# Where the sample stage's queries, constants, first keys and cache copies are issued, in a hybrid RG-LRU and windowed-attention step

## The chip, the core and the metric

The kernel runs on one core of a Trainium2 chip. The metric is the device time of one execution in microseconds (us), as the median of repeated runs. One execution was recorded by the hardware profiler; all rows below are from it. Engines are called PE (matrix products), DVE (vector), ACT (scalar functions), POOL (general) and SP, which in this kernel only issues transfers (DMAs). POOL and ACT issue DMAs too.

## The reference

One mixer layer is computed for a prompt of 2048 tokens and for 8 sequences with 8 new tokens each, which have caches. Cut to what matters:

```python
def dilated_group_sample(q, k, v, kv_buf, bias, dil):
    L = kv_buf.shape[1]                       # 128, 512, 2048 for the groups 0, 1, 2
    kc = jnp.concatenate([kv_buf[:, :, 0], k], axis=1)
    vc = jnp.concatenate([kv_buf[:, :, 1], v], axis=1)
    idx = L + jnp.arange(T)[:, None] - dil * jnp.arange(129)[None, :]   # dil 1, 4, 16
    s = jnp.einsum('bthe,btjhe->bthj', q, kc[:, idx]) * ATTN_SCALE + bias.T
    p, lse = softmax_stats(s, valid)
    o = jnp.einsum('bthj,btjhe->bthe', p, vc[:, idx])
    new_buf = jnp.stack([kc, vc], axis=2)[:, T:]      # the cache, shifted by 8 tokens
    return o, lse, new_buf

def mixer_layer(...):
    z = rms_norm(x, g_norm) @ w_in            # split in xa, ga, q, k, v, gb, gm
    hs, h_last = rg_lru(causal_conv(xa), h0, ...)
    ya = (hs * silu(ga)) @ w_lru_proj
    # three groups of 4 heads: banded attention for the prompt, the above for the samples
    yb = (merge of the groups * silu(gb)) @ w_attn_proj
    gates = sigmoid(gm + b_merge)
    y = x + (gates[:1024] * ya + gates[1024:] * yb) @ w_out
```

The caches of the samples are inputs, and the caches shifted by the 8 new tokens are outputs.

## The kernel before

The kernel is one hand-ordered program: each engine takes its instructions in the order of the code, and semaphores order the engines among each other. Its stages follow one another in time:

- The attention stage, 0 to about 1130 us: 12 heads of 17 units each (the loop variable is `i`). PE projects and computes the banded attention of the prompt.
- The gate of the attention output, then eight RG-LRU blocks, to about 1652 us.
- `gm_block(f)` for f = 0 to 15, to about 2061 us. Each f computes 128 of the merge gates' columns in five column tiles: 24 matmuls (`zT`, L763) into a PSUM tile, a sigmoid by ACT (L992), which empties the tile into gt, and a store to DRAM (Gsc, issued by ACT). Four PSUM tiles take turns. The weights of each f are loaded on SP (`wzr`, L683), cast by ACT and split by a subtraction on DVE (`wz`, L94 and L95). Between the tiles stands the attention of the samples: for f of 1 and more, one entry of the list `plan` is taken after each tile and its functions are called. The stretch f = 1 to 15 (1675 to 2061) is called the sample stage here.
- The output projections (L1424, L1480, L1512), to the end.

The attention of the samples has these pieces. `kmake` makes the key products of a group: `init` loads the first keys (kt, L156), `queries` loads the queries (qs, L146), and `go` does two products on DVE (kjk, L179), and loads the next keys. In the sample stage the group is 0, with four query tiles at first and four more in `go`, which go into the same buffers. `sload` and `sload_k` load scores of the new tokens and of the cached keys that other stages computed (SA, L1057, L1058; SCt, L1040, L1047). `scores` and `news` (L1066, L1072, L1075) put them together on DVE, with the constants MK, NI and relb, which `prep` loads. `v2_p` copies the normalised P for the values of group 2 (L1126). `v2_load(n)` loads cached values into one of six buffers (v, L1145), `v2_mul(n)` multiplies them by P on ACT (L1149), and `v2_acc(n)` adds them on DVE (L1155). `v1_p` sends P of group 1 through DRAM (PSC, L1134, on POOL). `v_conv` casts and splits values that `v_mm` multiplies on PE (vt, then OT at L1214).

`copy()` issues one of 184 transfers from a cache to its output (L110, on SP; 176 of them have 480 KB). It is called at fixed places of the attention stage, of the RG-LRU blocks and of `gm_block`, and does nothing when none is left. Before the change 94 are issued in the attention stage, 80 in the RG-LRU blocks, five in `gm_block(0)` and five in `gm_block(1)`.

The lines that issue the transfers at the beginning of the sample stage are these:

```python
    sload(2)
    sload_k(2)
    prep()
    for i in range(6):
        v2_load(i)
    G.kq = kmake(mp, 0, 2)
    plan += [[] for _ in range(70)]
    ...
    at_(1, G.kq.init, G.kq.queries)
```

Of the kernel before, what the change touches and what calls it, by code (L numbers as in the profile page):

```python
# [21 lines left out]
NS = 64  # L22
# [12 lines left out]
def raw(ap, off, dims):  # L35
    return bass.AP(ap.tensor, ap.offset + off, dims)
# [6 lines left out]
def program(tc, I, O, C, upto=99, debug=False):  # L43
    nc = tc.nc
    es = ExitStack()
    G = K()
# [4 lines left out]
    PE, ACT, DVE, POOL = nc.tensor, nc.scalar, nc.vector, nc.gpsimd  # L51
    dma = nc.sync.dma_start
# [9 lines left out]
    QS = sd("QS", [3, NS, 512])  # L62
# [16 lines left out]
    def pool(stack, name, **kw):  # L79
        return stack.enter_context(tc.tile_pool(name=name, bufs=1, reuse_waits="tile", **kw))  # L80
# [26 lines left out]
    def copy(n=1):  # L107
        for _ in range(n):
            if copies:
                i = dma(*copies.pop())  # L110
                if not G.manual:
                    tc.keep_in_program_order(i)
# [4 lines left out]
    def kmake(p, g, ntile):  # L117


        q = K()  # L120
        q.g = g
        q.SC = p.tile([128, 256], F32, name="SCk", tag="SCk", bufs=1)
        jk = p.tile([128, 128], mybir.dt.bfloat16, name="kjk", tag="kjk", bufs=1)
        kts, qts = {}, {}
        if g == 2:
            seq = [(n, 0) for n in range(64)]
            out = lambda n, t, h: h * 64 + n
        elif g == 1:
            seq = [(n, t) for n in range(32) for t in range(2)]
            out = lambda n, t, h: t * 128 + h * 32 + n  # L130
        else:
            seq = [(n, t) for half in range(2) for n in range(8) for t in range(half * 4, half * 4 + 4)]
            out = lambda n, t, h: t * 32 + h * 8 + n
        tiles = [seq[i][0] for i in range(len(seq)) if i == 0 or seq[i][0] != seq[i - 1][0]]

        def q_load(t):
            tag, bufs = ("qb", "q4")[t % 2] if g == 0 else "qs", (2, 2, 1)[g]
            qts[t] = p.tile([128, 512], F32, name="qs", tag=tag, bufs=bufs)
            if g == 2:
                for a in range(2):  # L140
                    dma(qts[t][a * NS:(a + 1) * NS], QS[2])
            elif g == 1:
                for b in range(8):
                    dma(qts[t][b * 16:(b + 1) * 16], raw(QS, (NS + b * 8 + 4 * t) * 512, [[0, 4], [512, 4], [1, 512]]))
            else:
                dma(qts[t], raw(QS, t * 512, [[8 * 512, 8], [0, 16], [1, 512]]))  # L146

        def k_load(i):
            if i < len(tiles):
                n = tiles[i]  # L150
                kts[i] = p.tile([128, 512], F32, name="kt", tag="kv", bufs=ntile)
                if g == 2:
                    for a in range(2):
                        dma(kts[i][a * NS:(a + 1) * NS], G.cache[2][:, (n * 2 + a) * 16:(n * 2 + a) * 16 + 8, 0].rearrange("b t h e -> b t (h e)"))
                else:
                    dma(kts[i], G.cache[g][:, n * 16:(n + 1) * 16, 0].rearrange("b t h e -> b t (h e)"))  # L156

        q.n, q.tile, q.half, q.left = 0, 0, 0, 2 * len(seq)

        def init():  # L160
            for i in range(ntile):
                k_load(i)

        def queries():
            for t in range((4, 2, 1)[g]):
                q_load(t)

        def go():
            q.left -= 1
            n, t = seq[q.n]  # L170
            if q.half == 0 and q.n and seq[q.n - 1][0] != n:
                q.tile += 1
                kts.pop(q.tile - 1)
            if q.half and q.tile and seq[q.n - 1][0] != n:
                k_load(q.tile + ntile - 1)
            for h in ((0, 1), (2, 3))[q.half]:
                c = slice(h * 128, (h + 1) * 128)
                o = out(n, t, h)
                DVE.tensor_tensor_reduce(jk, kts[q.tile][:, c], qts[t][:, c], 1.0, 0.0, ALU.mult, ALU.add, q.SC[:, o:o + 1])  # L179
            if g == 0 and q.half and 28 <= q.n < 32:  # L180
                q_load(t + 4)
            q.half ^= 1
            if q.half == 0:
                q.n += 1
            if q.left == 0:
                dma(SCs[g], q.SC)
        q.init, q.queries, q.go = init, queries, go
        return q
# [113 lines left out]
    def w_load(hd_, k):  # L302
        g, h = hd_
        hd = g * 4 + h
        wr = ap_.tile([128, 384], F32, name="wr", tag="wraw", bufs=4)
        src = win[k * 128:(k + 1) * 128, C_Q:C_GB].rearrange("p (s c) -> p s c", s=3)[:, :, hd * HD:(hd + 1) * HD]
        dma(wr.rearrange("p (s c) -> p s c", s=3), src)
        Wr[hd_, k] = wr
# [227 lines left out]
    for i in range(N + 3):  # L536
# [91 lines left out]
        if nh:  # L628
# [11 lines left out]
            if ph == 13:  # L640
# [1 line left out]
                w_conv(nh, 1, DVE)  # L642
                w_load(nh, 4)
                w_load(nh, 5)
        if i > 17 and i % 2:
            copy()
        if i == 115:
            k_flush()
# [368 lines left out]
    mp = pool(sms, "mp")  # L1017
    BF16 = mybir.dt.bfloat16
    relb = mp.tile([NS, 96], F32, name="relb")
    NI = mp.tile([NS, 11, NS], BF16, name="NI")  # L1020
    MK = mp.tile([NS, 3, NS], BF16, name="MK")
# [4 lines left out]
    Zc = [None]  # L1026

    def prep():
        dma(relb, I["rel_bias"][0:8].rearrange("b h -> (b h)").unsqueeze(0).to_broadcast([NS, 96]))
        dma(NI, C["ni"])  # L1030
        dma(MK, C["mk"])
        dma(SEL, C["sel"])
        for z in Zs:
            POOL.memset(z.bitcast(F32), 0.0)

    def sload_k(g):
        S = SCg[g] = mp.tile([NS, 512], F32, name="SCt", tag="PT")
        if g == 2:
            for a in range(2):
                dma(S[:, a * 256:(a + 1) * 256], SCs[2, a * NS:(a + 1) * NS])  # L1040
            return
        for t in range(8):
            if g == 1:
                src = SCs[1].rearrange("(b m r) (u c) -> u r b m c", b=8, r=4, u=2)[t // 4, t % 4]
            else:
                src = SCs[0].rearrange("(b s) (t c) -> t b s c", b=8, t=8)[t]
            dma(S[t:NS:8].rearrange("b (m c) -> b m c", c=(32, 128)[g]), src)  # L1047

    def sload(g):
        SA = SAs[g] = mp.tile([NS, 4, 192], F32, name="SA", tag="SA", bufs=2)  # L1050
        br = SA[:, :, 0:128]
        o = g * 4 * 128 * NBX + 127
        if g == 0:
            for h in range(4):
                dma(br[:, h], raw(Dsc, o + h * 128 * NBX, [[0, 8], [NBX - 1, 8], [1, 128]]))
        else:
            dma(br, raw(Dsc, o, [[0, NS], [128 * NBX, 4], [1, 128]]))  # L1057
        dma(SA[:, :, 128:192], SN[g * 4:g * 4 + 4].rearrange("h p k -> p h k"))  # L1058
# [63 lines left out]
    SEL = mp.tile([128, 2, NS], F32, name="SEL")  # L1122
# [14 lines left out]
    def v2_load(n):  # L1137
        if n < 96:
            v2s[n] = mp.tile([128, 4, 128], F32, name="v2", tag="v2", bufs=6)
        if 64 <= n < 96:  # L1140
            dma(v2s[n].rearrange("p h e -> p (h e)"), G.cache[1][:, (n - 64) * 16:(n - 63) * 16, 1].rearrange("b t h e -> b t (h e)"))
        if n < 64:
            for a in range(2):
                src = G.cache[2][:, (n * 2 + a) * 16:(n * 2 + a) * 16 + 8, 1].rearrange("b t h e -> b t (h e)")
                dma(v2s[n][a * NS:(a + 1) * NS].rearrange("p h e -> p (h e)"), src)  # L1145
# [119 lines left out]

    sload(2)
    sload_k(2)
    prep()
    for i in range(6):
        v2_load(i)  # L1270
    G.kq = kmake(mp, 0, 2)
    plan += [[] for _ in range(70)]

    def at_(n, *fs):
        plan[n].extend(fs)
# [3 lines left out]
    while len(kts) < G.kq.left:  # L1279
        t = kts[-1] if kts else 3  # L1280
# [11 lines left out]
        at_(mmt[i] - 1, P(v_conv, i))  # L1292
    T = mmt[-1]
    assert T + 1 < 68
    at_(1, G.kq.init, G.kq.queries)
    for i in range(2):
        at_(1 + i, P(states, i))
    at_(2, P(scores, 2), P(news, 2, range(4)), P(sload, 1), P(sload_k, 1))
# [5 lines left out]
    for i in range(98):  # L1304
        t = 6 + i * 60 // 98
# [296 lines left out]
```

## Time and profile before

| what | before |
|---|---|
| median of 3 runs | 2537.51 us (2537.02 to 2538.25) |
| the profiled execution, its own time | 2537.17 us |
| its span, first to last instruction | 2535.4 us |
| mean granted clock of PE | 0.995 |
| PE, DVE, ACT, POOL busy | 2482.5, 1543.3, 1081.6, 557.1 us |
| PE idle in the sample stage (1675 to 2061) | 386.00 - 363.45 = 22.55 us |

The span is the time between the first and the last recorded instruction; the execution's own time is 1.8 us longer. Busy times are sums over the span, and an engine that is busy part of the time can still be the one that another waits for at one place. The granted clock is a share of PE's full clock: 1.00 is 2.4 GHz, 0.50 is 1.2 GHz.

### The profile page before, as it was taken

The numbers are of one execution on the slowest core, as the hardware profiler recorded it, in microseconds if no ns is written. First come the engines' busy times: TensorE is split into PE (matmuls) and PEld (weight loads), VectorE is DVE, ScalarE is ACT, GpSimd is POOL, SyncE is SP. The second block draws the span as 40 slices with busy tenths as digits, with TensorE's granted clock in tenths as the row PEclk, the third lists the DMA queues.
The fourth block names the chain that finished last, engine by engine and source line by source line (L and its number), as shares of the span: only waits on it lengthen the run. The fifth ranks groups of instructions, "written<-read, shape, count | busy, mean of one in ns | idle before, by whom it ended". The sixth has DMA issues, their size and how long they took to land. (4 is left out here: it accounts for less than half of the span.)

```text
span 2535.4 us, 44585 instructions
## 1 busy us (share of the span) xinstructions
PE 2482.5 (98%) x15178; PEld 2337.5 (92%) x15178; DVE 1543.3 (61%) x4805; ACT 1081.6 (43%) x3318; POOL 557.1 (22%) x889
## 2 busy tenths in 40 slices
PE   7999999999999999999999999998998999999999
PEld 7999999999999999999999898997898899989988
DVE  6744686777786777646676677735776623433322
ACT  5633454443554443444465655544566511211110
POOL 3423322222212221213233343320000112200000
PEclk9999999999999999999999999999999999999999
DMA  5453564554553443327734333445664589533332
GB/s 145 118 123 99 140 187 136 163 167 143 160 162 106 123 118 96 111 73 227 216 131 156 130 116 124 141 136 192 193 206 153 160 234 333 188 107 127 109 123 67
DMA packets 311000, 376.30 MB, mean 148 GB/s; under 512 B 54912, under 2 KB 254639, under 8 KB 307932
## 3 DMA queue, kind: packets, MB, share of 16 engines
q1 hardware_dynamic: 285076, 338.42, 44.3%
q0 software_dynamic: 14176, 17.71, 2.6%
q10 hardware_dynamic: 11520, 17.31, 1.9%
q8 instruction: 120, 1.97, 0.3%
q14 instruction: 108, 0.88, 0.1%
HBM read 295.45 MB, written 168.33 MB: 183 GB/s over the span
## 5 line engine op out<-in xcount | busy, mean ns | idle before, releaser
L336 PE MATMUL z<-w,RH 128*128 128x384 f32 (+1 forms) x3088 | 888.7, 349 | 4.9 <-POOL w L317 1.7
L763 PE MATMUL zt<-RH,wz 128*128 128x384 f32 (+2 forms) x2560 | 700.6, 357 | 14.2 <-ACT gt L992 8.6
L336 PEld LDWEIGHTS z<-w,RH 128*128 128x128 f32 (+1 forms) x3088 | 553.2, 188 | 14.0 <-POOL w L317 5.9
L763 PEld LDWEIGHTS zt<-RH,wz 128*128 128x128 f32 x2560 | 466.3, 190 | 59.7 <-ACT gt L992 10.3
L336 PE MATMUL z<-w,RL 128*128 128x384 f32 x1544 | 520.8, 337 | 0.1
L763 PE MATMUL zt<-RL,wz 128*128 128x384 f32 (+2 forms) x1280 | 455.0, 355 | 0.0
L336 PEld LDWEIGHTS z<-w,RL 128*128 128x128 f32 x1544 | 291.7, 189 | 0.8 <-DVE RL L95 0.5
L763 PEld LDWEIGHTS zt<-RL,wz 128*128 128x128 f32 x1280 | 243.1, 190 | 22.3
L179 DVE CUSTOM_DVE_ANT_0 kjk<-kt,qs 128x128 bf16<-128x128 f32 x768 | 226.7, 295 | 60.3 <-DMA kt<-in_cache_kv_w 19.4
L408 ACT ACTIVATE P<-P,o 128x128 f32<-128x128 f32 (+1 forms) x192 | 88.9, 463 | 312.7 <-DVE o L407 312.7
L345 ACT ACTIVATE jk<-z 128x128 bf16<-128x128 f32 (+1 forms) x408 | 112.8, 277 | 249.4 <-PE trc L376 185.4
L95 DVE TENSOR_TENSOR KQ<-trc,KQ 128x256 fp32r<-128x256 f32 x192 | 81.4, 424 | 199.0 <-ACT KQ L94 198.8
L347 POOL TENSOR_SCALAR ss<-ss 128x2 f32<-128x2 f32 (+1 forms) x204 | 44.6, 219 | 706.0 <-ACT jk L345 663.2
L1480 PEld LDWEIGHTS zt<-y1t,w_wlo 128*128 128x128 f32 x1536 | 190.3, 192 | 0.6
L1480 PE MATMUL zt<-y1t,w_wlo 128*128 128x256 f32 (+1 forms) x1536 | 190.6, 287 | 0.0
L1512 PE MATMUL zt<-w_wo,mt 128*128 128x512 f32 x672 | 162.0, 395 | 0.0
L1512 PEld LDWEIGHTS zt<-w_wo,mt 128*128 128x128 f32 x672 | 126.2, 188 | 30.4
L348 POOL TENSOR_TENSOR rs<-ss,neghalf 128x2 f32<-128x2 f32 (+1 forms) x204 | 142.3, 697 | 17.0
L1149 ACT ACTIVATE v<-v,P 128x128 f32<-128x128 f32 x256 | 80.7, 390 | 78.7 <-DMA v<-in_cache_kv_w 52.4
L434 DVE TENSOR_REDUCE o<-op 128x128 f32<-128x256 f32 x192 | 80.6, 420 | 44.8 <-PE op L429 44.7
L94 ACT CAST mt<-g 128x256 fp32r<-128x256 f32 x72 | 27.1, 388 | 188.8 <-DVE g L1483 173.6
L1514 DVE TENSOR_TENSOR xr<-zt,xr 128x512 f32<-128x512 f32 (+1 forms) x34 | 23.5, 692 | 136.9 <-PE zt L1512 132.2
(286 smaller groups left out, 4239.4 us busy)
## 6 DMA issues: line engine op xcount, KB each, us to landing
out_kv_s<-in_cache_kv_w SPq DMA_DIRECT2D x176, 480.0 KB
xt<-in_x_prompt SPq DMA_DIRECT2D x48, 512.0 KB
wr<-in_w_in SPq DMA_DIRECT2D x96, 192.0 KB
kt<-in_cache_kv_w SPq DMA_DIRECT2D x128, 128.0 KB
wzr<-in_w_in SPq DMA_DIRECT2D x32, 512.0 KB
v<-in_cache_kv_w SPq DMA_DIRECT2D x128, 128.0 KB
Osc<-o SPq DMA_DIRECT2D x192, 65.0 KB
ot<-Osc SPq DMA_DIRECT2D x32, 390.0 KB
```

Of the source, the lines that this page charges most:

```text
L95: eng.tensor_sub(l, src, h.bitcast(F32))
L179: DVE.tensor_tensor_reduce(jk, kts[q.tile][:, c], qts[t][:, c], 1.0, 0.0, ALU.mult, ALU.add, q.SC[:, o:o + 1])
L336: PE.matmul(u.z[0:m, :], (RH, RL, RH)[p][:, k, u.cols], Wt[(u.g, u.h), k][:, (0, 0, 1)[p], :], start=(i == 0), stop=(i == 23))
L345: ACT.activation(jk[0:m, :], z[0:m, i * 128:(i + 1) * 128], AF.Square, accum_out=u.ss[0:m, i:i + 1])
L347: POOL.tensor_scalar(u.ss[0:m, :], u.ss[0:m, :], 1.0 / HD, EPS, ALU.mult, ALU.add)
L348: POOL.tensor_tensor(u.rs[0:m, :], u.ss[0:m, :], neghalf[0:m, :], ALU.pow)
L408: ACT.activation(u.P[:, 0:n], u.P[:, 0:n], AF.Exp, bias=u.o[:, 128:129], scale=-1.0, accum_out=u.o[:, 129:130])
L434: DVE.tensor_reduce(u.o[:, 0:128], u.op.rearrange("p a b -> p b a"), AX.X, ALU.add)
L763: PE.matmul(z[:, 0:n], w[:, (0, 1, 0)[p], k, :], (RH, RH, RL)[p][:, k, c0:c0 + n], start=(i == 0), stop=(i == 23))
L1149: ACT.activation(v2s[n][:, h], v2s[n][:, h], AF.Copy, scale=P2[:, h, n:n + 1])
L1480: PE.matmul(z[:, 0:n], wl[k][:, (0, 1, 0)[p], f, :], y1s[c * 8 + k][:, (0, 0, 1)[p], 0:n], start=(i == 0), stop=(i == 23))
L1512: PE.matmul(z[0:m, :], ms_[k][:, (0, 0, 384)[p] + o:(0, 0, 384)[p] + o + m], wo[k][:, (0, 1, 0)[p], e * 4:(e + 1) * 4, :].rearrange("p k c ...
```

## The change

Four things are moved. The queries of group 0, both the first four and the four that replace them later, are issued by POOL. The constants MK, relb, NI and SEL are issued by POOL too. The first two key loads are issued before `prep` and the value loads, and the queries within `prep`, where both stood in the second entry of `plan`. And `copy()` is called at 12 more places of the attention stage (i = 20, 36, ..., 196), so that no copy is left for `gm_block`; the last two places in the RG-LRU blocks stay empty as well.

```diff
@@ q_load(t), group 0
             else:
-                dma(qts[t], raw(QS, t * 512, [[8 * 512, 8], [0, 16], [1, 512]]))
+                POOL.dma_start(qts[t], raw(QS, t * 512, [[8 * 512, 8], [0, 16], [1, 512]]))
@@ the attention stage, once for each i
-        if i > 17 and i % 2:
+        if i > 17 and (i % 2 or i % 16 == 4):
             copy()
@@ prep()
-        dma(relb, I["rel_bias"][0:8].rearrange("b h -> (b h)").unsqueeze(0).to_broadcast([NS, 96]))
-        dma(NI, C["ni"])
-        dma(MK, C["mk"])
-        dma(SEL, C["sel"])
+        POOL.dma_start(MK, C["mk"])
+        POOL.dma_start(relb, I["rel_bias"][0:8].rearrange("b h -> (b h)").unsqueeze(0).to_broadcast([NS, 96]))
+        POOL.dma_start(NI, C["ni"])
+        G.kq.queries()
+        POOL.dma_start(SEL, C["sel"])
@@ before the sample stage
     sload(2)
     sload_k(2)
+    G.kq = kmake(mp, 0, 2)
+    G.kq.init()
     prep()
     for i in range(6):
         v2_load(i)
-    G.kq = kmake(mp, 0, 2)
...
-    at_(1, G.kq.init, G.kq.queries)
```

Behind this, a line of the changed kernel has a number one higher than before. On SP, at the beginning of the sample stage, the order before is this (SCt are scores, v values, wzr weights, kt keys, qs queries; out_kv_s is a copy):

```order
L1040 DMA SCt<-SCs 64x256 x2
L1029 DMA relb<-in_rel_bias 64x96
L1030 DMA NI<-c_ni 64x704
L1031 DMA MK<-c_mk 64x192
L1032 DMA SEL<-c_sel 128x128
L1145 DMA v_21087<-in_cache_kv_w 64x1x512 x2
...
L683 DMA wzr<-in_w_in 128x8x128
L110 DMA out_kv_s<-in_cache_kv_w 16x7680 x2
L156 DMA kt<-in_cache_kv_w 128x1x512 x2
L146 DMA qs<-QS 128x1x512 x4
```

The same place on SP in the changed kernel:

```order
L1058 DMA SA<-Dsc 64x4x128
L1059 DMA SA<-SN 64x4x64
L1041 DMA SCt<-SCs 64x256 x2
L156 DMA kt<-in_cache_kv_w 128x1x512 x2
L1146 DMA v_21106<-in_cache_kv_w 64x1x512 x2
...
L683 DMA wzr<-in_w_in 128x8x128
L1058 DMA SA<-Dsc 64x4x128
L1059 DMA SA<-SN 64x4x64
L1048 DMA SCt<-SCs 8x4x128 x8
```

The constants, the copies and the queries are gone from this list, and the keys stand ahead of the values; the next scores follow directly on the weights. On POOL, the order behind the last RG-LRU block (par, L930) is this before:

```order
L930 COPY par<-tt 128x1
L931 COPY par<-tt 128x8
L1034 MEMSET Z_21071 128x512
L1264 DMA out_conv_p<-hs 3x1024
L1264 DMA out_h_p<-hs 16x1x64
L1264 DMA out_conv_s<-hs 24x1024
L1264 DMA out_h_s<-hs 8x1024
L1134 DMA PSC<-pp 32x1x128 x8
L1135 DMA P_21074<-PSC 128x256
L95 TENSOR_TENSOR vt_23879<-vr,vt_23879 64x512
```

And in the changed kernel:

```order
L931 COPY par<-tt 128x8
L1029 DMA MK<-c_mk 64x192
L1030 DMA relb<-in_rel_bias 64x96
L1031 DMA NI<-c_ni 64x704
L146 DMA qs<-QS 128x1x512 x4
L1033 DMA SEL<-c_sel 128x128
L1035 MEMSET Z_21076 128x512
...
L1135 DMA PSC<-pp 32x1x128 x8
L1136 DMA P_21079<-PSC 128x256
L146 DMA qs<-QS 128x1x512 x4
L95 TENSOR_TENSOR vt_23879<-vr,vt_23879 64x512
```

POOL now has the eight new transfers directly behind its last RG-LRU work, and the four later query loads between PSC's return and its first work on vt. On SP, these later queries stood among loads of values and keys before:

```order
L156 DMA kt<-in_cache_kv_w 128x1x512
L146 DMA qs<-QS 128x1x512 x2
L1145 DMA v_22298<-in_cache_kv_w 64x1x512 x2
L146 DMA qs<-QS 128x1x512
L1145 DMA v_22356<-in_cache_kv_w 64x1x512 x2
L1145 DMA v_22359<-in_cache_kv_w 64x1x512 x2
L146 DMA qs<-QS 128x1x512
L156 DMA kt<-in_cache_kv_w 128x1x512
L683 DMA wzr<-in_w_in 128x8x128
```

In the changed kernel SP has the same loads of values, keys and weights there without the queries.

## Rows read from the trace of the kernel before

**Rows 1.** The page, busy us, share of the span and instructions of each engine:
```profile
PE 2482.5 (98%) x15178; PEld 2337.5 (92%) x15178; DVE 1543.3 (61%) x4805; ACT 1081.6 (43%) x3318; POOL 557.1 (22%) x889
```

**Rows 2.** Windows by stage: length, busy time of each engine, clock, DMA share, GB/s:
```profile
20.00:1130.00 1110.00, 1096.72 (x6976) 1067.87 (x6976) 765.39 (x2930) 496.93 (x2037) 281.35 (x572) 1.00 0.47 131
...
1675.00:2061.00 386.00, 363.45 (x1874) 326.60 (x1873) 235.35 (x889) 201.13 (x524) 24.37 (x42) 0.97 0.57 183
2061.00:2535.00 474.00, 470.09 (x3108) 433.49 (x3106) 162.39 (x341) 68.91 (x155) 49.76 (x47) 1.00 0.51 159
```

**Rows 3.** Waits of PE in 1640 to 2070: total, times, longest:
```profile
PE zt L763 <- ACT gt L992: 8.6, 4, 3.6
PE OT L1214 <- DVE vt L95: 6.8, 1, 6.8
PE zt L763 <- DVE wz L95: 5.6, 1, 5.6
```

**Rows 4.** Windows of the sample stage, then of its stretches at half clock:
```profile
1721.80:1845.10 123.30, 109.10 (x530) 96.48 (x529) 91.20 (x419) 68.90 (x194) 4.91 (x9) 0.94 0.57 186
1725.70:1732.50 6.80, 4.70 (x11) 3.74 (x12) 6.31 (x34) 6.00 (x20) 0.00 (x0) 0.50 0.30 97
1770.10:1773.50 3.40, 3.40 (x12) 3.40 (x12) 2.89 (x18) 2.92 (x10) 2.35 (x5) 0.51 0.60 189
1838.30:1841.70 3.40, 3.40 (x10) 2.63 (x9) 1.90 (x10) 2.87 (x9) 0.00 (x0) 0.50 0.66 232
```

**Rows 5.** Timeline of DVE: start, length, instruction, [idle before it <-releaser]:
```profile
1700.30 0.22 DVE L1072 TENSOR_TENSOR SA<-SA,MK 64x64 f32<-64x64 f32 x1 [5.16 <-DMA MK<-c_mk]
...
1721.35 0.29 DVE L179 CUSTOM_DVE_ANT_0 kjk<-kt,qs 128x128 bf16<-128x128 f32 x1 [18.19 <-DMA qs<-QS]
...
1726.53 1.22 DVE L95 TENSOR_TENSOR wz<-wzr,wz 128x1024 fp32r<-128x1024 f32 x1
```

**Rows 6.** Timeline of SP, which issues DMAs, 1679 to 1746:
```profile
1679.59 2.80 SPq L927 DMA_DIRECT2D Y<-sgl  x3
1682.45 2.82 SPq L110 DMA_DIRECT2D out_kv_s<-in_cache_kv_w  x3
...
1688.19 4.40 SPq L1040 DMA_DIRECT2D SCt<-SCs  x2
...
1699.36 7.80 SPq L1145 DMA_DIRECT2D v<-in_cache_kv_w  x12
1707.62 0.39 SPq L683 DMA_DIRECT2D wzr<-in_w_in  x1
...
1711.80 1.78 SPq L156 DMA_DIRECT2D kt<-in_cache_kv_w  x2
1713.62 8.75 SPq L146 DMA_DIRECT2D qs<-QS  x4
...
1744.19 1.31 SPq L1145 DMA_DIRECT2D v<-in_cache_kv_w  x2
```

**Rows 7.** Waits of the SP queue, 1684 to 1727:
```profile
SPq L146 <- DMA Gsc<-gt: 5.1, 1, 5.1
```

**Rows 8.** Timeline of ACT at three of its waits:
```profile
1714.57 1.05 ACT L94 CAST wz<-wzr 128x1024 fp32r<-128x1024 f32 x1 [7.68 <-DMA wzr<-in_w_in]
...
1748.37 1.28 ACT L1149 ACTIVATE v<-v,P 128x128 f32<-128x128 f32 x4 [13.45 <-DMA v<-in_cache_kv_w]
...
1836.13 1.28 ACT L1149 ACTIVATE v<-v,P 128x128 f32<-128x128 f32 x4 [7.56 <-DMA v<-in_cache_kv_w]
```

**Rows 9.** Waits of the SP queue, 1800 to 1830:
```profile
SPq L146 <- DVE SCk L179: 6.7, 3, 3.1
```

**Rows 10.** Timeline of POOL, 1682 to 1790:
```profile
1682.12 0.19 POOL L931 COPY par<-tt 128x8 f32<-128x8 f32 x1
...
1771.15 4.33 POOL L1134 DMA_DIRECT2D PSC<-pp  x8 [77.09 <-DVE pp L1131]
```

**Rows 11.** The page, a DMA queue: packets, MB, share of 16 engines over the span:
```profile
q1 hardware_dynamic: 285076, 338.42, 44.3%
```
## The prediction

> **What bounds the kernel now.** I read the page first: PE is busy 98% of the span [rows 1], so the time is PE's work plus the little that it idles, and another engine counts only where PE waits for it. Then I cut the span by stages [rows 2]. In the attention stage (20 to 1130 us) PE idles 1110.00 - 1096.72 = 13.3 us. In the sample stage (1675 to 2061) it idles 386.00 - 363.45 = 22.6 us, and the granted clock there is 0.97, where the other two stretches show 1.00. Behind it PE idles 3.9 us in 474, so what the sample stage gives back reaches the end of the program undiminished.
>
> PE's waits in the sample stage are few [rows 3]: once 5.6 us for the next converted weight (wz, from DVE), four times, 8.6 us in all, for ACT to empty a PSUM tile (gt), and once 6.8 us for converted cached values (vt). The first five, 14.2 us, lie between 1722 and 1842: PE is busy 109.10 us of those 123.30 [rows 4]. Three of the waits are followed by a stretch at a granted clock of 0.50 (the 1.2 GHz level); PE is busy 4.70, 3.40 and 3.40 us in them [rows 4]. Work at half the clock takes twice as long, so half of these 11.50 us, 5.75, is lost. The stalls therefore cost 14.20 + 5.75 = 19.95 us. That is the most the change can win in this place.
>
> What is late there? I followed the waits backwards. The converted weight is the subtraction on DVE that begins at 1726.53 [rows 5]. DVE takes its queue in order, and ahead of the subtraction stand the first key products (kjk, L179), which began only at 1721.35 after DVE had idled 18.19 us for the queries qs. The queries are the last of a long list on SP [rows 6]: three Y stores, three copies, scores, constants, twelve loads of values, weights, two copies, keys, and then qs from 1713.62. Those four queries alone held SP for 8.75 us, of which SP waited 5.1 us for an earlier transfer to land (a Gsc store, issued by ACT) [rows 7]. ACT suffers from the same lateness. It waits 13.45 us at 1748 for values [rows 8] which SP issued only from 1744.19 on, after the queries and the copies [rows 6]. PE has four PSUM tiles to run ahead in; when ACT is later than that, PE stops. The wait at 1837.9 has a second source: ACT waits 7.56 us for values until 1836.13 [rows 8], and SP had just stood 6.7 us in three waits of the later query loads, which need DVE to let go of a buffer, with value loads queued behind them [rows 9].
>
> **The change, part by part.** *Queries and constants on POOL.* POOL has finished its last RG-LRU work at 1682.31 [rows 10] and then needs only one memset and four stores until 1771. It now issues MK, relb, NI, four qs and SEL, eight DMAs. It issued eight small ones in 4.33 us at 1771, 0.54 each [rows 10]; SP's longest price for a query is 8.75 / 4 = 2.2 with its waits [rows 6]. I take about 0.6 (4.33 / 8 and a little), so the last is out by 1682.3 + 8 x 0.6 = 1687. On SP, the time from the first query's issue to the first key product was 1721.35 - 1713.62 = 7.7 us; with that landing time the queries are there at about 1695. At 2.2 us each they would be there at 1682.3 + 17.6 + 7.7 = 1707.6. The keys (two kt, 1.78 us) are now issued behind the scores (SCt). SP's list behind the Y stores ends its SCt now at 1692.59, 7.3 us after the copies end at 1685.27 [rows 6]. Starting at 1682.39, without the copies, even with all present waits, it comes to SCt 1689.7, kt 1691.5, values 1699.3, weight wzr 1699.7, where it is 1708.01 now. With fewer waits it is earlier.
>
> What DVE then sees: MK, for which it waited 5.16 us until 1700.30 [rows 5], lands before 1692; key products begin between 1695 and 1708 in place of 1721.35. The subtraction stands 1726.53 - 1721.35 = 5.2 us behind the first of them and also needs ACT's cast of wzr, which ended at 1715.62, 7.6 us after the issue [rows 6, 8]. So it is due at about 1708 by the weights, at the latest 1713 by the queries. PE wants it at 1722, and the first wait is gone by both bounds. What hides the work then is PE's own 22 us of column tiles.
>
> Next is ACT's chain. It multiplies values by P, which DVE copies between those key products, and then needs the values that SP issues at 1744.19. Of what stood between wzr and those loads, the copies (3.04 us and three later single ones), the keys and the 8.75 us of queries leave: 13.6 us from rows alone. With the 8.3 us by which wzr is earlier, the loads go out 21.9 us earlier, so 13.45 us of ACT's wait can vanish, and the three waits of PE behind it with it. They could stay if buffers and not SP's list hold the loads back; the six value buffers come free by ACT's multiplications, which themselves start earlier, and so I expect them to follow.
>
> The wait at 1837.9 costs 3.6 us and half of 3.40, 5.3 together. Its loads move up by at least the 6.7 us of waits, which are POOL's now, and by four issues; against them stand ACT's 7.56 us. POOL's own waits for the buffer hold up nothing that PE needs soon, since behind the four later queries POOL has only vt work at about 1950. I count this stall as removed as well, with less certainty.
>
> *Twelve copies into the attention stage.* Ninety-four copies stand there now, with 13.3 us of PE idle in total [rows 2]; if every bit of that were theirs, one would cost 0.14 us, and twelve 1.7. Below that lies nothing at all, since PE's waits there are for DVE or POOL work and the copies run beside them. I take the middle, 0.9. The upper bound is their full transfer time: SP's and ACT's queue moved 338.42 MB in 44.3% of the span of 16 engines [rows 11], so a copy of 480 KB occupies them 491,520 / 338.42e6 x 0.443 x 2535 = 1.6 us; twelve, all on the path, 19.6 us.
>
> *The wait for vt* (6.8 us) is not touched: its scores are loaded after the last key product, which PE's tile count sets. It should only move forward.
>
> **The sum.** 2537.17 us in the profiled execution, less 19.95, plus 0.9: 2518.1. The median of the runs is 0.34 above the profiled one, so I predict 2518.5.
>
> **A rule against it.** Eight POOL DMAs at 1771 were issued in 4.33 us while DVE was at work [rows 10], without a gap. The Trainium skill, "SBUF — State Buffer", section "Who interferes with whom", says that a DMA issued from GpSimd can be starved while DVE holds the port that they share, and advises SP or ACT as issuers. Taken at its worst here, POOL would issue nothing until DVE goes idle behind the work at 1703; then the queries land at 1703 + 4.8 + 7.7 = 1715.5, 5.9 us earlier than now. That is rival two below. The Trainium skill, "DMA: Bandwidth & Descriptors", section "Issuing engines are not separate DMA queues", says that spreading DMAs over issuers saves only issue time; that would be eight issues of 0.6, 4.8 us, of the same first wait. The 5.1 us that SP's queue stood waiting in front of a query speak for more than that.
>
> **The rivals.** *One: the stall at 1837.9 stays*, because the loads are held by buffers that DVE frees late. That leaves 5.3 us: 2523.8. *Two: only the first wait goes*, because queries come only some 6 us sooner or the values are held by buffers. It gains 5.6 + 4.70 / 2 = 7.95, and with 0.9 for the copies: 2530.5. *Three: the copies eat it.* At the full 1.6 us each the gain is used up: 2537.2 - 19.95 + 19.6 = 2536.8, no change. *Four, slower*: if each copy makes PE wait as long and a stretch at half clock follows (3.40 us busy, 1.7 lost, as behind the wait before 1770 [rows 4]), a copy costs 3.3 and twelve 39.6: 2537.5 - 19.95 + 39.6 = 2557. It decides from (19.95 + 5.1) / 12 = 2.1 us a copy on. The 94 present copies, at no more than 0.14, speak strongly against three and four. *Five: more is won*, because the wait for vt shrinks with a quieter stage: half of it, 3.4 and some clock, gives 2513.
>
> **How the numbers follow.** All five stalls gone (2516.5 to 2520.5): 0.58. One: 0.15. Two: 0.11. Five: 0.03. Three, or a gain that does not come for a reason I don't see: 0.07. Four, or a new wait of that size: 0.06. The measurement tells 0.2%, 5.1 us, from nothing. Faster by more: 0.58 + 0.15 + 0.11 + 0.03 = 0.87; within it 0.07; slower 0.06. The range from 2513 to 2530.5 takes in all cases of a gain and leaves out those two.
>
> **What would show it.** In the profile after, key products of the sample stage begin before 1708 and the subtraction ends before PE wants it; PE's waits for wz and gt between 1700 and 1845 are under 1 us together, and the granted clock there is 1.00. ACT's long waits for values at about 1748 and 1836 are gone. The wait for vt is still there, about 20 us earlier. The RG-LRU stage begins within 2 us of where it does now. I am wrong if PE idles more in the attention stage, each new copy beside a wait; if POOL's DMAs land late and qs still releases DVE after 1715; or if the loads of values move up and ACT waits all the same.

## The result, and the profile after

The changed kernel took 2514.42 us as the median of 5 runs (2513.91 to 2520.85), against 2537.51 us. The ratio is 0.9914, with a 95% interval of 0.9899 to 0.9928. A later comparison on another chip gave 0.9919 (0.9905 to 0.9933). The forecast was 2518.5, in a range of 2513 to 2530.5.

The profiled execution took 2513.91 us, 23.26 less than that of before. The windows of the changed kernel, with the columns of [rows 2], show where:

```profile
20.00:1130.00 1110.00, 1096.05 (x6964) 1066.57 (x6964) 764.51 (x2929) 497.58 (x2035) 281.59 (x571) 1.00 0.48 136
1675.00:2061.00 386.00, 381.56 (x2076) 347.30 (x2075) 245.11 (x906) 205.24 (x528) 35.34 (x58) 0.99 0.60 188
1700.00:1845.00 145.00, 145.00 (x758) 131.44 (x757) 106.69 (x482) 90.11 (x244) 7.34 (x13) 1.00 0.60 192
```

From 1700 to 1845 us PE is busy for all of the 145.00 us, at full clock. All five waits of [rows 3] and the three stretches at half clock of [rows 4] are gone. The waits of PE in 1640 to 2047 are down to one:

```profile
PE OT L1215 <- DVE vt L95: 4.3, 1, 4.3
```

It is the wait for vt, which was 6.8 us. ACT's longest wait for values between 1690 and 1840 us is 3.2 us now, where it was 13.45 [rows 8]. SP's timeline at the beginning of the sample stage answers to [rows 6]:

```profile
1682.69 0.32 SPq L927 DMA_DIRECT2D Y<-sgl  x1
1683.10 0.67 SPq L1058 DMA_DIRECT2D SA<-Dsc  x1
1683.82 0.63 SPq L1059 DMA_DIRECT2D SA<-SN  x1
1684.55 1.20 SPq L1041 DMA_DIRECT2D SCt<-SCs  x2
1685.84 1.34 SPq L156 DMA_DIRECT2D kt<-in_cache_kv_w  x2
1687.27 16.04 SPq L1146 DMA_DIRECT2D v<-in_cache_kv_w  x12
1703.41 0.40 SPq L683 DMA_DIRECT2D wzr<-in_w_in  x1
1703.86 1.11 SPq L1058 DMA_DIRECT2D SA<-Dsc  x1
1705.01 0.64 SPq L1059 DMA_DIRECT2D SA<-SN  x1
1705.76 7.56 SPq L1048 DMA_DIRECT2D SCt<-SCs  x8
...
1721.61 2.62 SPq L1146 DMA_DIRECT2D v<-in_cache_kv_w  x4
```

The second batch of values is issued at 1721.61, where it was 1744.19. The twelve first value loads, though, now hold SP for 16.04 us, where it was 7.80: with less in front of them they start 12 us sooner, and then SP waits between them for earlier transfers to land (Gsc 4.1 us, SCt 2.8, kt 1.2). POOL's timeline, which answers to [rows 10], has the eight new transfers directly behind its RG-LRU work:

```profile
1682.86 0.61 POOL L1029 DMA_DIRECT2D MK<-c_mk  x1
...
1684.50 2.46 POOL L146 DMA_DIRECT2D qs<-QS  x4
1686.89 0.65 POOL L1033 DMA_DIRECT2D SEL<-c_sel  x1
```

The first key product on DVE and the subtraction for PE's next weight, which answer to [rows 5]:

```profile
1695.83 0.29 DVE L179 CUSTOM_DVE_ANT_0 kjk<-kt,qs 128x128 bf16<-128x128 f32 x1 [0.20 <-DMA out_h_s<-hs]
...
1711.21 1.23 DVE L95 TENSOR_TENSOR wz<-wzr,wz 128x1024 fp32r<-128x1024 f32 x1 [8.68 <-ACT wz L94]
```

Both are well ahead of 1722, where PE waited for them before. What the subtraction waits for now is ACT's cast, and that for the landing of wzr.

### The profile page after: what moved, and what is told of

Read it like the earlier page. It is cut to its first block, busy times and chain, and to the rows that moved or that the text cites. A ratio compares the mean times of both kernels' runs of the same rounds, so it can differ in the third digit from the quotient of the medians.

```text
span 2512.1 us, 44593 instructions
## 1 busy us (share of the span) xinstructions
PE 2477.1 (99%) x15178; PEld 2333.8 (93%) x15178; DVE 1544.1 (61%) x4805; ACT 1083.5 (43%) x3318; POOL 565.1 (22%) x901
## 3 DMA queue, kind: packets, MB, share of 16 engines
q10 hardware_dynamic: 11520, 17.31, 1.9%
## 4 chain that ended last, share of the span: by engine, by line
PE 87%; DMA 4%; DVE 3%; ACT 2%; issue 2%; POOL 1%; SPq 0%; ACTq 0%; POOLq 0%; DVEq 0%
PE z L336 28%; PE zt L763 28%; PE zt L1481 8%; PE zt L1513 7%; PE zt L1425 3%; PE zt L534 3%; PE zga L891 2%; PE trx L248 1%; PE op L428 1%; PE S L406 1%; PE tre L416 1%; PE trc L376 1%; DMA wr<-in_w_in 1%; DMA xt<-in_x_prompt 1%; PE trc L377 1%
## 5 line engine op out<-in xcount | busy, mean ns | idle before, releaser
L179 DVE CUSTOM_DVE_ANT_0 kjk<-kt,qs 128x128 bf16<-128x128 f32 x768 | 227.5, 296 | 37.0 <-DMA kt<-in_cache_kv_w 13.8
```

## The experiments

Repeated runs of one kernel here lie up to 11 us apart, and the intervals of the ratios are about 0.0014 (3.5 us) to either side. Differences under some 4 us are therefore not told apart by the times, and the traces have to speak. Ratios are to the kernel before on the same chip.

**The copies put back** (u_copies): the line of the attention stage as before, all else as changed.

```diff
-        if i > 17 and (i % 2 or i % 16 == 4):
+        if i > 17 and i % 2:
             copy()
```

> The change with the twelve extra copies of the attention stage taken back, so that ten copies stand in the first two blocks of gm_block again, five of them on SP between the first weights and the key loads. My theory (the stalls came from what stood on SP ahead of queries, weights and values): five single issues and two pieces of traffic, some 5 us on SP, which the slack of the changed kernel holds; 2514 to 2518 us, no PE wait over 1 us before 1845 us. Rival (the copies' traffic made the loads late): most of the 20 us comes back, 2528 to 2534, with PE waits on gt and wz again.

Measured: 2534.51 us, ratio 0.9983 (0.9973 to 0.9992). Most of the gain is gone; my theory expected 2514 to 2518. SP's timeline in this kernel shows how:

```profile
1682.43 0.32 SPq L927 DMA_DIRECT2D Y<-sgl  x1
1682.81 3.05 SPq L110 DMA_DIRECT2D out_kv_s<-in_cache_kv_w  x3
1686.65 0.66 SPq L1058 DMA_DIRECT2D SA<-Dsc  x1
1689.43 0.62 SPq L1059 DMA_DIRECT2D SA<-SN  x1
1690.15 6.28 SPq L1041 DMA_DIRECT2D SCt<-SCs  x2
1697.90 2.02 SPq L156 DMA_DIRECT2D kt<-in_cache_kv_w  x2
...
1708.53 0.39 SPq L683 DMA_DIRECT2D wzr<-in_w_in  x1
1709.16 7.02 SPq L110 DMA_DIRECT2D out_kv_s<-in_cache_kv_w  x3
...
1722.71 10.13 SPq L1048 DMA_DIRECT2D SCt<-SCs  x8
```

From the end of the Y stores to the first keys it is 1697.90 - 1682.75 = 15.2 us here, and 1685.84 - 1683.01 = 2.8 in the change. From the end of wzr's issue to the eight SCt loads it is 13.8 us here and 2.0 there. So three copies in front of the scores cost SP 12.3 us and three behind the weights 11.8, of which their own rows are 3.05 and 7.02. A row of several issues runs from the first to the last, waits between them included: 5.2 of the 7.02 us are waits of the copies themselves for earlier values and weights to land. Most of the rest is waiting in front of the issues behind the copies, for stores of ACT (Gsc) by the profile, which infers what a wait ends with:

```profile
SPq L1041 <- DMA Gsc<-gt: 5.2, 1, 5.2
SPq L1059 <- DMA Gsc<-gt: 4.4, 1, 4.4
```

ACT waits for values again, 15.21 us until 1745.12, and PE's waits are back, though not the one for wz:

```profile
PE zt L763 <- ACT gt L992: 11.2, 3, 6.3
PE OT L1215 <- DVE vt L95: 5.9, 1, 5.9
```

**The first queries and constants on SP again** (u_pool): the four constants and the first four queries by `dma`, at the same place of the code.

```diff
-        POOL.dma_start(MK, C["mk"])
+        dma(MK, C["mk"])
...
-                POOL.dma_start(qts[t], raw(QS, ...))
+                (POOL.dma_start if t >= 4 else dma)(qts[t], raw(QS, ...))
```

> The change with the constants and the first four queries issued by SP again, at the same place of the code (behind the first keys, ahead of the values); later queries stay on POOL. My theory: SP issues eight more transfers and waits for earlier ones to land in front of them, as the 8.75 us for four queries showed before; values and the first weights go out 8 to 14 us later, and the first wait of PE (wz) or the first ones on gt return in part: 2517 to 2526. Rival (the order alone does it, the issuer only saves 5 us of issue time, which is hidden): 2514 to 2516, no PE wait before 1845.

Measured: 2520.25 us, ratio 0.9922 (0.9909 to 0.9935). The time lies in my theory's range, and the delay on SP came as forecast: the weights go out 7.2 us later than in the change (1710.57) and the second batch of values 8.2 us later (1729.85). But PE's waits, which were to give the time, did not return: it has one of 0.5 us before 1900. What is longer in the profiled run is the wait for vt, of 9.6 us:

```profile
PE OT L1215 <- DVE vt L95: 9.6, 1, 9.6
PE OT L1215 <- POOL Z L1205: 2.0, 2, 1.6
PE zt L763 <- ACT gt L992: 0.5, 1, 0.5
```

The interval overlaps with those of the change. Who issues the first queries is not shown to matter once the copies are gone.

**The later queries on SP again** (u_reload): the same line with `t < 4` for POOL.

> The change with the four later queries issued by SP again, among the loads of values. My prediction put the stall at 1837.9 us (3.6 us and 1.7 of half clock) down to these: by it 2518 to 2520 with one PE wait on gt near 1815 to 1840. Rival (that stall was the rest of ACT's lateness from the first 50 us, and with that gone the four waits on SP are held by the slack): 2514 to 2515, no such wait.

Measured: 2519.79 us, ratio 0.9923 (0.9911 to 0.9935). The time lies in the range of my prediction's reading (2518 to 2520), but the one wait that was to make it did not come. SP does wait in front of these queries, 8.7 us, longer than the 6.7 of before [rows 9]:

```profile
SPq L146 <- DVE SCk L179: 8.7, 3, 3.5
```

Yet PE has no wait at all between 1700 and 1900 us. And with the copies back, but these queries on POOL (u_copies), ACT's wait for values and the stall behind it are there, 5 us earlier in the program's time than before:

```profile
1831.06 1.28 ACT L1150 ACTIVATE v<-v,P 128x128 f32<-128x128 f32 x4 [7.10 <-DMA v<-in_cache_kv_w]
...
1832.86 0.73 PE L763 MATMUL zt<-RH,wz 128*128 128x512 f32 x2 [3.32 <-ACT gt L992]
```

So the later queries on SP do not make that stall by themselves, and it does not need them. The rival's reading, that ACT was late from the first 50 us on, fits both runs.

**The keys behind the values again** (u_keys): `init` called by the second entry of the plan.

```diff
     G.kq = kmake(mp, 0, 2)
-    G.kq.init()
     prep()
...
+    at_(1, G.kq.init)
```

> The change with the two first key loads issued by the second entry of the plan again, behind values and weights. My theory: keys land some 15 to 20 us later, near 1712, the key products on DVE begin then instead of at 1696, and the wz subtraction behind them still ends before PE wants it at 1722; 2514 to 2517. Rival (the early keys are what wins, since DVE's queue stands behind them): the first wait of PE on wz returns, 2520 to 2530.

Measured: 2517.57 us, ratio 0.9913 (0.9899 to 0.9926), the change's own. The first key product begins at 1709.18, the subtraction for wz at 1713.58, and PE waits for neither.

**The copies alone** (o_copies): the kernel before with the changed line of the attention stage and nothing else.

> The kernel before with one part of the change alone: twelve more copies in the attention stage, so that none is left for gm_block. Constants and queries stay on SP, keys behind the values. New theory, after the copies' undoing gave back most of the gain (in front of the scores, and between the first weights and the next scores, ten copies hold SP's queue, which issues nothing else while it waits for them): this part alone wins most, 2518 to 2526, with part of the first wait left. My prediction's theory (the queries and constants on SP are the main delay): 2530 to 2535.

Measured: 2522.49 us, ratio 0.9935 (0.9920 to 0.9949). This one part brings 16.7 us. Its profiled run, at 2515.38 us the shortest of its six, does not show where the 7 us up to the median lie. In it constants and queries are on SP; the four queries hold SP for 4.51 us, where they held it for 8.75 [rows 6]. DVE still idles 17.03 us for them, but the first key product comes at 1711.08, the subtraction at 1717.55, and PE does not wait for wz:

```profile
1701.94 4.51 SPq L146 DMA_DIRECT2D qs<-QS  x4
...
1711.08 0.29 DVE L179 CUSTOM_DVE_ANT_0 kjk<-kt,qs 128x128 bf16<-128x128 f32 x1 [17.03 <-DMA qs<-QS]
```

PE's waits in 1640 to 2070 are these:

```profile
PE OT L1214 <- DVE vt L95: 7.0, 1, 7.0
PE OT L1214 <- POOL Z L1204: 2.1, 1, 2.1
PE zt L763 <- ACT gt L992: 0.6, 1, 0.6
```

**The copies put back, on POOL** (cp_pool): as the first experiment, with the copies of gm_block issued by POOL.

```diff
-                i = dma(*copies.pop())
+                i = (POOL.dma_start if G.cpool else dma)(*copies.pop())
...
     G.wr = wgr
+    G.cpool = True
     gm_block(0, ...
```

> The change with ten copies back in the first two blocks of gm_block, as in the run that undid them, but issued by POOL instead of SP. The transfers are the same and at the same time; SP's queue is free of them. If they cost through SP's queue (SP stands in front of the next issue until an earlier transfer has landed): 2514 to 2520. If they cost through their traffic (they delay the landing of values and weights): 2528 to 2536, as with the copies on SP.

Measured: 2522.85 us, ratio 0.9941 (0.9928 to 0.9955). It lies between the two theories. Off SP's queue the same copies cost about 6 us against the change, in place of some 17 (0.9983 less 0.9914 to 0.9919). But the queue isn't all. SP's value loads of this kernel take much longer in their turn:

```profile
1688.91 24.72 SPq L1148 DMA_DIRECT2D v<-in_cache_kv_w  x12
```

That is 24.72 us for the twelve, with 16.04 in the change; SP's waits between them name SA (7.9 us) and kt (6.5) transfers that had not landed. PE waits 4.7 us for gt. So the copies also slow what is in flight beside them, whoever issues them: the first four queries, which POOL issues in all three kernels, land 7.2 us (median) behind their issue in the change, 10.6 with the copies on SP and 12.1 with the copies on POOL. The Trainium skill, "DMA: Bandwidth & Descriptors", section "Issuing engines are not separate DMA queues", says that transfers of all issuers run on the same engines and interleave; this run agrees. The same section of the Trainium skill says that another issuer saves only the time that the issuing takes. Here it saved more: 0.9983 against 0.9941 is 10.7 us for ten copies, whose single issues on SP and POOL take 0.5 to 0.8 us each. SP still stood in front of loads, but the eight SCt loads went out at 1715.55 in place of 1722.71 and the second batch of values at 1731.19 in place of 1739.94.

**The price of the twelve copies in the attention stage** (drop10): the copies that would be left for gm_block are cleared from the list, so that ten pieces of two cache outputs are not written.

> The change without the twelve extra calls in the attention stage, and with the ten copies that would be left for gm_block left out of the computation (ten pieces of a cache output are not written). It has two more copies in the last RG-LRU block than the change. Against the change its time gives the price of the twelve copies in the attention stage: by my sum 0.9 us in all, at most 1.7, so 2512 to 2514.5; by the rival (their full transfer time, 1.6 us each) 2495.

Measured: 2515.29 us, ratio 0.9910 (0.9895 to 0.9925), with the change at 0.9914 and 0.9919. The twelve copies have no price that these times can show, which tell differences of some 4 us. Attention's PE is busy 1096.02 us of 1110 in this run, 1096.05 in the change.

**A copy at every unit** (dense): `if i > 17:` at the same place, 184 copies in the attention stage in place of 106.

> The change with a copy at every unit of the attention stage from 18 on, so that all 184 stand there (78 more than in the change) and none in the RG-LRU blocks or gm_block. If a copy costs next to nothing beside attention (0.14 us at most, by my sum): no more than 11 us above the changed kernel, and rather 0 to 5. If a copy costs its transfer time of 1.6 us there as soon as they stand close: 125 us above it.

Measured: 2523.87 us, ratio 0.9939 (0.9923 to 0.9955), 5.9 us above the change on the same chip, 0.08 us for each of the 78. The intervals overlap, but the window of the attention stage shows PE idle for 20.0 us, and 13.6 in the change beside it, and these 6.4 us are about the difference in time:

```profile
20.00:1130.00 1110.00, 1089.97 (x6904) 1061.07 (x6904) 758.76 (x2912) 490.76 (x2015) 276.54 (x564) 1.00 0.57 168
```

**The first queries ten microseconds later** (late_q): `queries` called behind the stores of the states, still on POOL.

```diff
-        G.kq.queries()
...
         at_(1 + i, P(states, i))
+    at_(2, G.kq.queries)
```

> The change with POOL issuing the first four queries behind the four stores of the RG-LRU states, some 10 us later than in the change (near 1695 in place of 1685). My prediction gave the queries slack until 1715 to land, so: no change against the changed kernel, key products begin near 1703, no PE wait on wz. Rival (the early queries are what wins): a PE wait on wz or gt returns, 4 to 10 us above it.

Measured: 2517.87 us, ratio 0.9918 (0.9905 to 0.9932); the change beside it had 2517.98 and 0.9919. POOL issues the queries from 1695.14 on, and DVE now waits for them:

```profile
1703.52 0.29 DVE L179 CUSTOM_DVE_ANT_0 kjk<-kt,qs 128x128 bf16<-128x128 f32 x1 [7.37 <-DMA qs<-QS]
```

PE does not wait for it. There is slack of at least ten microseconds, as the forecast had it.

**The change again** (r_after), as the reference for late_q, dense and the last one:

> The changed kernel once more, on the same chip as the three below, so that they have a reference. All theories: 0.990 to 0.993 of the kernel before.

Measured: 2517.98 us, ratio 0.9919 (0.9905 to 0.9933). Its profiled execution took 2516.85 us. The wait for vt was 5.9 us in it, and 4.3 in the first profile: the size of this wait differs from run to run. And the wait behind it, for converted P from POOL, which the first profile does not have, is here:

```profile
PE OT L1215 <- DVE vt L95: 5.9, 1, 5.9
PE OT L1215 <- POOL Z L1205: 2.0, 1, 2.0
```

**Three more transfers on POOL** (best):

```diff
-                dma(SCs[g], q.SC)
+                (POOL.dma_start if g == 0 else dma)(SCs[g], q.SC)
...
-            dma(S[t:NS:8].rearrange("b (m c) -> b m c", c=(32, 128)[g]), src)
+            (POOL.dma_start if g == 0 else dma)(S[t:NS:8].rearrange("b (m c) -> b m c", c=(32, 128)[g]), src)
...
-        dma(sm[NS:128, 2], sw)
+        POOL.dma_start(sm[NS:128, 2], sw)
```

> The change, and three more transfers on POOL: the store of group 0's key products (SCs), the eight loads of them behind it (SCt), and the store of the softmax weights (sm). On SP the last two hold up value loads behind them, for 5.9 and 10.0 us in the trace of the changed kernel, shortly ahead of its last large wait of PE (vt, 4.3 us, and 6.21 us of work at half clock behind it, 3.1 lost). If that wait comes from these loads: 2507 to 2510. If it comes from the softmax's own chain on DVE and ACT: 2513 to 2515, the wait unchanged.

Measured: 2517.54 us, ratio 0.9914 (0.9899 to 0.9929): no gain. The values do come earlier, but the softmax on DVE now waits for its scores instead, and the wait for vt is 4.3 us as before:

```profile
1909.63 1.10 DVE L1067 TENSOR_TENSOR SA<-SCt,SA 64x512 f32<-64x512 f32 x1 [5.02 <-DMA SCt<-SCs]
```

**The first conversion of values earlier** (early_vt):

```diff
+        if i:
-        at_(mmt[i] - 1, P(v_conv, i))
+            at_(mmt[i] - 1, P(v_conv, i))
...
-    plan[kl + 3] = [P(scores, 0), P(soft_a, 0), weights] + plan[kl + 3]
+    plan[kl + 3] = [P(v_conv, 0), P(scores, 0), P(soft_a, 0), weights] + plan[kl + 3]
```

> The change with the first conversion of cached values (v_conv(0), ACT's cast and DVE's subtraction) moved from the entry kl + 6 of the plan to the head of entry kl + 3, ahead of the last scores and their softmax. The loads on POOL left PE's wait for vt as it was, and the rows there show the cast and subtraction standing in ACT's and DVE's order behind 20 us of softmax and multiplications, though they need none of it. If that order is the cause, PE's wait of 4.3 us and the half clock behind it (3.1 us lost) go: 5 to 8 us below the changed kernel. If ACT's lateness itself is the cause, a wait on gt takes its place, and the time stays.

Measured: 2515.53 us, ratio 0.9902 (0.9887 to 0.9916), the lowest ratio of all kernels here; the change on the same chip had 2517.98. The intervals overlap, so the gain of 2.5 us is not settled. In its profiled run, at 2509.80 us the shortest of the five, the wait for vt is gone, as the first theory has it, but the next product now waits for its own conversion, on POOL:

```profile
PE OT L1215 <- POOL vt L95: 3.4, 1, 3.4
PE OT L1215 <- POOL Z L1205: 1.6, 1, 1.6
```

## Why the prediction came out right, and where its reasons did not

**The sum.** It had -19.95 for the five stalls and their half clock, and +0.9 for the copies: 2518.1 for the profiled execution, which took 2513.91. The stalls went in full: the five waits, 14.2 us, are gone, and PE's busy time in the whole span fell from 2482.5 to 2477.1 us, 5.4, where I had 5.75 for the half clock. The sample stage started 0.6 us later than before (the last Y store on SP ends at 1683.01, before at 1682.39), which leaves at most that much for the copies in attention. The 4.2 us that are missing are in the main a term that I set to nothing: PE's wait for vt shrank from 6.8 to 4.3, and the wait of 1.6 us behind it (for converted P, from POOL) did not occur. That one stands in the same view of the kernel before, and I left it out of [rows 3]:

```profile
PE OT L1214 <- POOL Z L1204: 1.6, 1, 1.6
```

Together they are 4.1 us: 19.95 + 4.1 - 0.6 makes 23.45, and 23.26 was measured. In the repetition the two waits were 5.9 and 2.0, 7.9 us in place of 8.4, and its profiled execution, 2516.85, lies nearer to the 2518.1 of the sum. So these 4.1 us are not shown to come from the change; that the first measurement was so low is chance in some measure, and the forecast of an unchanged wait is not refuted.

**The first step, what is late.** I held that the queries stood last in SP's list and so made DVE late, PE's weight late, and ACT late. The list was the right place. But I took the queries, the constants and the copies by the lengths of their own issue rows: 8.75 us for four queries, 2.82 and 3.04 for the copies at the two places. That is the step that failed. The lengths in [rows 6] say who stands in the queue at the moment, and not who made it stand. With the copies put back SP lost 12.3 and 11.8 us at these places, 24.1 together; 10.1 of it is in the copies' own rows, and 14.0 in and between the rows of other transfers (SA, SCt), mostly in waits for an earlier one to land. In the kernel before without these copies (o_copies) the same four queries took 4.51 us on SP, and the first key product came at 1711.08, early enough. The copies are thus worth 16.7 us alone, and the other three parts 4.6 us with the copies left in place (0.9983). That these three are worth 4 to 5 us more on top of the copies is likely from 0.9935 against 0.9914 to 0.9919, but the intervals overlap. Taken back one at a time, with the copies gone, none of them changed the time by more than the runs can tell, and no trace shows which of them such a gain would come from.

**ACT's chain.** I had the second batch of values 21.9 us earlier; it came 22.6 us earlier (1721.61). The sum was right by two errors: wzr was issued 4.2 us earlier and not 8.3, since the twelve loads of values took twice as long, and the way from wzr to these loads shrank by 18.4 us and not by 13.6. With queries and keys moved but the copies there, the batch went out at 1739.94, and ACT's waits brought PE's back. What the step lacked was an experiment in thought: each cause removed alone.

**The stall at 1837.9.** Its cause, as I put it, was SP's 6.7 us in front of the later queries. Two runs refute it: queries on SP without copies, no stall; queries on POOL with copies, a stall of 3.3 behind ACT's wait of 7.10. That it was a remainder of ACT's earlier lateness fits all runs; that is argued, not shown by a run of its own.

**POOL.** I had 0.6 us for each issue and the last out at 1687; it was 2.46 for four, and 1687.54. The key products began at 1695.83 (forecast 1695 to 1708). The Trainium skill's rule in "SBUF — State Buffer", section "Who interferes with whom", that a DMA issued by GpSimd (POOL) can be starved while DVE holds the port they share, did not show. DVE was busy for only 0.59 of the 4.68 us, so this is no test of the rule; nor was it needed, as late_q's slack shows.

**The rivals.** The first (the stall at 1837.9 stays) and the second (only the first wait goes) did not come. The third and fourth, the price of copies in attention, are refuted at 1.6 us each by drop10 and by dense (0.08 each). The 1.6 us rest on [rows 11], which I took for SP's and ACT's queue together. ACT's Gsc stores are 17.3 MB in all, the size of another queue on the profile's page (q10, 17.31 MB), so q1 is likely SP's alone; the 1.6 us do not change by it. The fifth, a shorter wait for vt and 2513, is what the first profile shows in part, and the repetition hardly: the median of 2514.42 lies between it and the main case (2516.5 to 2520.5), and the repetition's ratio, 0.9919 of 2537.51 or 2517.0, lies within the main case. That removing the copies alone could bring most of the gain was not among my rivals.

## What to carry to other kernels

When a queue that issues in order is late, do not take the causes by the length of each issue's row: a large transfer can make the small ones behind it wait, and the time appears under their names. Ask instead how the queue would run without each of them. Large transfers that nobody waits for belong where the queue has room, here in a stage where one cost 0.08 us or less, and not in front of short loads on which an engine depends. A total that comes out right can rest on two wrong shares; taking back one part at a time shows it.

## What the runs showed of the hardware that I had not expected

Twelve value loads that were issued 12 us earlier, with nothing large in front of them, took SP 16.04 us in place of 7.80. Issued so early, they were held by landings (SP's waits in front of them name Gsc, SCt and kt transfers, up to 2.8 us at a time). Beside copies issued from POOL the same twelve took 24.72 us. Copies in one issuer's queue also delayed the transfers of another: POOL's first four queries landed 7.2 us (median) behind their issue without the copies, and 10.6 with the copies on SP.
